# A planned encoder layer: one gate moved between two mixers, two heads kept on chip, and the last product's order changed

## The chip, the cores and the metric

The kernel runs on one core of a Trainium2 chip. Five engines work side by side, each through its own list of instructions in order: TensorE (PE, with its weight loads PEld), VectorE (DVE), ScalarE (ACT), GpSimd (POOL) and SyncE (SP), which here issues nearly all DMAs. The metric is the device time of one execution in microseconds (us), the median of several runs; lower is better.

## The reference

One layer is computed for 1024 prompt rows and 32 sample rows (T = 1056 columns in all), with 1024 channels, 8 heads of 64 in each of two mixers, and a feed-forward width of 4096:

```
z = rmsnorm(x) @ w_in                    # q, k, v of both mixers, indexer, two gates
o_a = softmax attention over the 256 best keys per row (mixer A)
o_b = stick-breaking attention (mixer B)
m = sigmoid(gate_a) * (o_a @ w_branch_a) + sigmoid(gate_b) * (o_b @ w_branch_b)
h = x + m @ w_out
y = h + square(relu(rmsnorm(h) @ w_up)) @ w_down
```

The outputs are y for both groups and the new keys and values.

## The kernel before

All matrix products are made to near full precision with three passes: a value is split into a high part and a low rest (on ACT a cast to the high part, on POOL or DVE a subtraction for the rest), and `three` (line 514) multiplies high by high, high by low and low by high. One 128 by 512 slab of weights is a unit: a DMA into `wst`, the cast to `wh`, the subtraction to `wl`.

**What sets the order.** The program is not written in the order in which it runs. Every call is recorded as a node; a planner (`Plan`) gives each node an estimated cost and issues on each engine, among the nodes that are ready by its reckoning, the one of the lowest rank: FAST, PREP, MAIN, FILL, SLOW. Matmuls of products are FILL, so that PE takes them only where the matmuls of attention aren't ready. What comes out is one fixed list for each engine; on the chip each list runs in order.

**The attention stage.** Mixer B's 8 heads come first, then mixer A's twice over: pass 0 for the first 512 rows, pass 1 for the other 512. For a 128-row tile PE multiplies q by k (bank `s`, three of them); mixer A then takes on DVE the masked maximum (which empties the bank), on ACT the exponential, on DVE the reciprocal of its sum, on POOL the scaling of `p`; PE transposes `p` (bank `t`), ACT and DVE split the transposed tile (`tt`), PE multiplies by v (bank `o`), and `halves` adds the two halves of the result into a tile `o`, which goes by DMA to `do` in DRAM. Mixer B uses sigmoids in place of the exponential.

**What fills PE there.** The 16 gates (8 for each mixer) are products of 72 matmuls each: 24 of 512 columns and 48 of 272 (`gate`). Four run before the stage, four at its start, and `GATES_BESIDE` says how many are recorded after each of mixer B's heads: six. The last two are in `self.raw`: they are recorded among mixer A's heads and stored without their sigmoid, which is taken later, where the gate is loaded again (`gated` and `merge`); so ACT needs no sigmoid between the exponentials of mixer A. Beside mixer A's heads stand 26 pieces of filling: the two raw gates and 24 branch products (`branch_b0`, `branch_b1`, `branch_a0`, 8 each), dealt out by `FILL_AHEAD` and `FILL_BESIDE`.

**The merge.** `load_o` brings the heads' results back from `do` in pairs of heads, splits them (cast on ACT, subtraction on POOL), and the branch products of the second half (`w_ba` by `xl`) follow, then `w_out`, then the feed-forward part.

**Down.** The last product takes seven forms of the hidden layer (B11, T1 to T4, B21, B22: a scheme of seven block products in place of eight), read back from `du` in DRAM. Its phases before are: B11 over all 16 blocks p; (T2, T3, B22) over blocks 0 to 7, then over 8 to 15, called here three-0 and three-1; B21 over all 16; (T1, T4) over 0 to 7 and over 8 to 15, called two-0 and two-1. In each phase q runs over 4 pairs of output rows. At q = 0 the phase loads its u (one DMA, cast and subtraction for each form and block), and keeps them until q = 3; there are 24 places for them (`slots`), taken in turn over the tiles ml, oa, xl and mh. B11 and B21 need 16, a three 24, a two 16. For each q and four blocks a three also makes three sets of weights from four loads (`us<-w_down`) by four additions and subtractions on DVE, while B11 and B21 just load a unit. `finish` multiplies a finished part of y by the norm and adds h, loaded into one of `self.hs` (4 places).

Of the kernel before, what the change touches and what calls it, by code (L numbers as in the profile page):

```python
# [28 lines left out]
H = 8  # L29
# [15 lines left out]
MIDS = 1  # L45
FILL_AHEAD = 1
GATES_BEFORE, GATES_FIRST = 4, 4
GATES_BESIDE = (1,1,1,1,1,1,0,0)
FILL_BESIDE = (0,1,1,1,2,2,2,2,2,2,2,2,2,2,2,1)
FWORDS = 2500  # L50
PA_BANKS = ('s', 'pj', 's', 's', 'pj')
TOPK = (("a", [2, 3, 4, 7], (7,), 0), ("b", [5, 6, 8], (5, 6), 16))
# [55 lines left out]
class Plan:  # L108
# [3 lines left out]
    def __init__(self, nc, tc):  # L112
        self.nc, self.tc = nc, tc
        self.tensor, self.vector = Issuer(self, PE, nc.tensor), Issuer(self, DVE, nc.vector)
        self.scalar, self.gpsimd = Issuer(self, ACT, nc.scalar), Issuer(self, POOL, nc.gpsimd)
        self.sync = Issuer(self, SP, nc.sync)
        self.either = Issuer(self, EITHER, nc)
        self.nodes, self.mem, self.rings = [], {}, {}
        self.members, self.banks, self.onchip = {}, set(), set()
        self.floors = {"left": 0.0, "right": 0.0, None: 0.0}  # L120
        self.free = [0.0] * 5
        self.now = [[] for _ in range(5)]
        self.later = [[] for _ in range(5)]
        self.pipe = 0.0
        self.port = {DVE: (0.0, 0.0), POOL: (0.0, 0.0)}
        self.table = None
        self.level = [2]
        self.hold = None
# [22 lines left out]
    def open(self, name, side="left", space=None):  # L151
        st = ExitStack()
        kw = {"space": space} if space is not None else {"side": side}
        if space is not DRAM:
            kw["reuse_waits"] = "tile"
        pool = st.enter_context(self.tc.tile_pool(name=name, bufs=1, **kw))
        p = (pool, st, side if space is None else None, name)
        self.members[name] = []
        return p

    def close(self, *pools):
# [7 lines left out]
    def tile(self, pool, shape, dtype, name, tag=None, bufs=1, fine=False):  # L169
        tag = tag or name  # L170
        kw = {} if pool[2] is None and pool[3].startswith("d") else {"tag": tag, "bufs": bufs}
        t = pool[0].tile(shape, dtype, name=name, **kw)
        words = 1
        for s in shape[1:]:
            words *= s
        if dtype in SMALL:
            words = -(-words * SMALL[dtype] // 4)
        if kw:
            ring = self.rings.setdefault((pool[3], tag), [])
            old = ring[-bufs].touched if len(ring) >= bufs else ()  # L180
            psum = pool[3].startswith("ps") and not fine
            m = Mem(1 if psum else 4, 1 if psum else words, old, self.floors[pool[2]])
            ring.append(m)
        else:
            m = Mem(1, words * shape[0])
        self.mem[t.tensor.name] = m
        if pool[3].startswith("ps"):
            self.banks.add(t.tensor.name)
        if kw:
            self.onchip.add(t.tensor.name)  # L190
        self.members[pool[3]].append(m)
        return t
# [267 lines left out]
class Layer:  # L460
# [732 lines left out]
        nc.vector.tensor_sub(tt[:m, 1, :n], pt[:m, :n], tt.bitcast(F32)[:m, 0, :n])  # L1193
        return tt

    def halves(self, po, o):

        nc = self.nc
        nc.scalar.copy(o, po[64:128])
        nc.vector.tensor_add(o, po[0:64], o)  # L1200

    def rooms(self, is_a):

# [3 lines left out]
    def attend(self, h, is_a, passes=(0, 1)):  # L1207

        nc, at = self.nc, self.att
        g = h if is_a else H + h  # L1210
        kk = nc.tile(at, [128, SEQ], F32R, "k", bufs=3)
        v = nc.tile(at, [128, 8, 128], F32R, "v", bufs=3)
        dk = self.dk[g].rearrange("s e t -> (s e) t")
# [25 lines left out]
        for i in passes:  # L1239
            o = nc.tile(at, [64, 512], F32, "o", bufs=2)  # L1240
            for t0 in (4 * i + 2, 4 * i):
# [8 lines left out]
                for j0 in range(0, t0 + 2, 2):  # L1250
# [6 lines left out]
                    for j in (j0, j0 + 1):  # L1257
                        lo = 128 if j > t0 else 0
                        s0 = 256 * (j - j0)
                        for z in range(2):  # L1260
                            nc.tensor.matmul(
                                po[:, lo:256], v[:, j], parts[:, z, s0:s0 + 256 - lo],
                                start=j + z == 0, stop=j + z == t0 + 2)
                self.halves(po, o[:, c:c + 256])
            with nc.rank(FAST):
                nc.sync.dma_start(self.do[g, :, 512 * i:512 * i + 512], o)
            self.mid = self.mid[1:] + [len(nc.nodes) - 1]

    def attend_new(self, u, is_a):
# [79 lines left out]
    def load_o(self, o, g, groups):  # L1349

        nc = self.nc
        for e in range(4):
            for i in groups:
                lo, hi = ((0, W1), (W1, T))[i]
                h, l = o[i][:, e], o[i][:, 4 + e]
                with nc.rank(PREP):
                    nc.sync.dma_start(
                        l.bitcast(F32), self.do[2 * g + 2 * e:2 * g + 2 * e + 2, :, lo:hi].rearrange("g e t -> (g e) t"))
                    nc.scalar.copy(h, l.bitcast(F32))
                    nc.gpsimd.tensor_sub(l, l.bitcast(F32), h.bitcast(F32))  # L1360

    def branch(self, name, e, o, done, parts):

# [272 lines left out]
    def down(self, late, form):  # L1636
# [4 lines left out]
        slots = self.ring([  # L1641
            v for z in homes for v in self.temps(flat(z), z.shape[1] * z.shape[2] // T, 0, T)])
        raws = self.ring(self.temps(late[0], 4, 0, 512) + self.temps(late[1], 4, 0, 512))
        self.hs = self.ring(self.temps(self.ft, 4, 0, 512))
        half = T // 2

        def raw(q, p, r, c):
# [55 lines left out]
                for r, c in ((1, 1), (0, 1), (1, 0)):  # L1703
                    d(r, c, True)

        for fs, weights, blocks, after in (
                ((B11,), one(0, 0), (range(16),), after1),
                ((T2, T3, B22), weights6, (range(8), range(8, 16)), after6),
                ((B21,), one(0, 1), (range(16),), after2),
                ((T1, T4), weights5, (range(8), range(8, 16)), after5)):  # L1710
            for b, block in enumerate(blocks):
                u = {}
                for q in range(4):
                    tags = [next(self.turn) for _ in fs]
                    ps = [[self.bank(t)[:, :n] for n, _ in QUADS] for t in tags]
                    for p0, ws in [(p0, weights(q, p0 // 4)) for p0 in range(block[0], block[-1], 4)]:
                        for f, w, bank in zip(fs, ws, ps):
                            wh, wl = w()
                            if q == 0:
                                u.update({(f, p): load(f, p) for p in range(p0, p0 + 4)})  # L1720
                            for i, (n, lo) in enumerate(QUADS):
                                cs = slice(i * 256, i * 256 + n)
                                with nc.rank(FILL):
                                    for s in range(4):
                                        ks = slice(s * 128, s * 128 + 128)
                                        uh, ul = (z[:, cs] for z in u[f, p0 + s])
                                        self.three(bank[i], wh[:, ks], wl[:, ks], uh, ul,
                                                   p0 + s == block[0], p0 + s == block[-1])
                    for i, (n, lo) in enumerate(QUADS):

                        def d(r, c, done=False, q=q, n=n, lo=lo):
                            cs = slice(lo + c * n, lo + c * n + n)
                            if done:
                                return self.finish(2 * q + r, cs)
                            return self.pick(self.yy, 2 * q + r, cs)

                        with nc.rank(FAST):
                            after(b, d, *(z[i] for z in ps))

    def finish(self, e, cs):  # L1740

# [93 lines left out]
```

## Time and profile before

| | |
|---|---|
| median of 3 runs | 1705.32 us (1704.97 to 1709.24) |
| the profiled execution's own time | 1703.88 us |
| its span, first to last instruction | 1702.1 us |
| PE busy | 1671.8 us (98%) |
| DVE, ACT, POOL busy | 1349.7, 942.4, 847.7 us |

In the rows further on, busy time of PE is modelled: a matmul's record lasts until its result is out, while the next one already runs, so a full PE still may not be at its fastest. The issue interval, from the start of one matmul to the start of the next, tells more. Every record names line 440, where the planner calls the operation, so the tiles tell the place: `s`, `t`, `o` are attention, `pj` with `xh` and `xl` a gate or a branch, `pj` with `og` a branch of the first half; `a`, `b`, `c` and `pj` are the four banks of the later stages.

### The profile page before, as it was taken

How to read it: one execution, taken by the hardware profiler on the slowest of the kernel's cores; microseconds unless marked ns; L12 is line 12 of the kernel's file. 1: busy time of each engine (PE TensorE's matmuls, PEld its weight loads, DVE VectorE, ACT ScalarE, POOL GpSimd, SP SyncE). 2: the span in 40 equal slices, each digit the busy share in tenths (PEclk: the TensorE clock that was granted, in tenths of full speed). 3: DMA queues.
4: the chain of work that ended last, by engine and by line, in shares of the span. 5: the costliest groups of instructions: out<-in, count | busy, mean ns of one | idle time of the engine just before them, and what ended most of it. 6: DMA issues, size and time to landing. Idle time of an engine off the chain costs nothing.

```text
span 1702.1 us, 34820 instructions
## 1 busy us (share of the span) xinstructions
PE 1671.8 (98%) x12242; PEld 1591.3 (93%) x12242; DVE 1349.7 (79%) x2846; ACT 942.4 (55%) x2019; POOL 847.7 (50%) x699
## 2 busy tenths in 40 slices
PE   8999999999999999899999999999999999999998
PEld 7998999999999998798999999999999999989998
DVE  8777899987477888876666549999988879888756
ACT  7556888764376776877754555333333544425431
POOL 5432332343386676456668648433333556656420
PEclk9999999999999999999999999999999999999999
DMA  7234453355573636778855644444443687756744
GB/s 257 83 104 125 140 154 121 103 157 149 156 213 94 188 97 166 197 237 241 241 178 160 182 122 134 156 140 140 140 150 130 225 274 237 271 161 235 252 131 149
DMA packets 182575, 289.00 MB, mean 170 GB/s; under 512 B 30976, under 2 KB 62176, under 8 KB 182400
## 3 DMA queue, kind: packets, MB, share of 16 engines
q1 hardware_dynamic: 182112, 286.43, 54.4%
q8 instruction: 97, 1.59, 0.4%
q14 instruction: 78, 0.64, 0.1%
q10 hardware_dynamic: 288, 0.34, 0.1%
HBM read 193.52 MB, written 93.07 MB: 168 GB/s over the span
## 4 chain that ended last, share of the span: by engine, by line
PE 85%; DVE 8%; issue 2%; DMA 2%; ACT 1%; POOL 1%; SPq 0%; DVEq 0%; ACTq 0%; POOLq 0%
PE pj L440 35%; PE c L440 11%; PE b L440 10%; PE a L440 10%; PE s L440 10%; PE o L440 5%; PE t L440 5%; DVE junk L440 2%; DVE y L440 1%; DVE mh L440 1%; DVE us L440 1%; POOL wl L440 0%; SPq L440 0%; DVE wl L440 0%; DVE small L440 0%
## 5 line engine op out<-in xcount | busy, mean ns | idle before, releaser
L440 PE MATMUL pj<-xl,wh 128*128 128x272 f32 (+2 forms) x1200 | 335.5, 312 | 0.0
L440 POOL TENSOR_TENSOR wl<-wst,wh 128x512 fp32r<-128x512 f32 x160 | 231.5, 1455 | 200.8 <-ACT wh L440 195.1
L440 PE MATMUL pj<-xh,wh 128*128 128x272 f32 (+1 forms) x768 | 251.6, 328 | 0.0
L440 PE MATMUL pj<-xh,wl 128*128 128x272 f32 (+1 forms) x768 | 250.8, 327 | 0.2 <-POOL wl L440 0.2
L440 PEld LDWEIGHTS pj<-xl,wh 128*128 128x128 f32 x1200 | 212.9, 188 | 10.5
L440 ACT CAST wh<-wst 128x512 fp32r<-128x512 f32 x213 | 130.4, 620 | 132.0 <-PE a L440 21.9
L440 PEld LDWEIGHTS pj<-xh,wl 128*128 128x128 f32 x768 | 144.5, 188 | 11.1 <-POOL wl L440 0.5
L440 PEld LDWEIGHTS pj<-xh,wh 128*128 128x128 f32 x768 | 144.6, 188 | 10.2 <-DVE gz L440 0.3
L440 POOL TENSOR_TENSOR p<-p,rem 128x383 f32<-128x383 f32 (+8 forms) x66 | 101.8, 1562 | 45.3 <-DVE rem L440 34.3
L440 DVE TENSOR_TENSOR tt<-t,tt 128x512 fp32r<-128x512 f32 (+2 forms) x168 | 101.4, 621 | 26.4 <-ACT tt L440 25.5
L440 POOL TENSOR_TENSOR wl<-y,wh 128x512 fp32r<-128x512 f32 x49 | 73.2, 1496 | 95.9 <-ACT wh L440 92.8
L440 DVE TENSOR_TENSOR_SCAN rem<-rem,first 128x384 f32<-128x384 f32 (+8 forms) x66 | 113.9, 1748 | 7.5 <-ACT rem L440 6.3
L440 ACT CAST tt<-t 128x512 fp32r<-128x512 f32 (+2 forms) x168 | 86.9, 539 | 42.0 <-PE t L440 34.6
L440 ACT CAST wh<-y 128x512 fp32r<-128x512 f32 x79 | 49.1, 622 | 105.9 <-issue 23.0
L440 ACT ACTIVATE junk<-score,cand 128x1024 bf16<-128x1024 f32 (+2 forms) x93 | 97.0, 1043 | 12.3 <-DVE cand L440 10.7
L440 PE MATMUL s<-k,q 128*128 128x512 f32 (+4 forms) x384 | 97.9, 353 | 5.6 <-DVE nb L440 3.0
L440 ACT CAST wh<-us 128x512 fp32r<-128x512 f32 x64 | 39.6, 622 | 114.1 <-PE pj L440 27.6
L440 PE MATMUL o<-tt,v 128*128 128x256 f32 (+1 forms) x640 | 98.4, 279 | 0.8 <-DVE o L440 0.4
L440 PEld LDWEIGHTS o<-tt,v 128*128 128x128 f32 x640 | 89.9, 189 | 6.3 <-DVE o L440 0.7
L440 DVE TENSOR_SCALAR_CACHE_REDUCE junk<-score,cand 128x384 bf16<-128x384 f32 (+1 forms) x124 | 92.9, 749 | 3.1
L440 PE MATMUL t<-ident,p 128*128 128x128 f32 (+1 forms) x596 | 90.9, 275 | 0.2 <-DVE tt L440 0.2
L440 POOL TENSOR_TENSOR wl<-us,wh 128x512 fp32r<-128x512 f32 x33 | 49.7, 1515 | 72.6 <-ACT wh L440 72.6
(359 smaller groups left out, 5610.3 us busy)
## 6 DMA issues: line engine op xcount, KB each, us to landing
us<-w_down SPq DMA_DIRECT2D x80, 256.0 KB, 3.0
q<-dq SPq DMA_DIRECT2D x64, 256.0 KB, 4.5
du<-y SPq DMA_DIRECT2D x56, 264.0 KB, 2.5
du<-us SPq DMA_DIRECT2D x56, 264.0 KB, 2.5
y<-w_up SPq DMA_DIRECT2D x44, 256.0 KB, 2.7
k<-dk SPq DMA_DIRECT2D x40, 256.0 KB, 5.0
v<-dv SPq DMA_DIRECT2D x40, 256.0 KB, 4.3
xl<-du SPq DMA_DIRECT2D x35, 264.0 KB, 5.2
```

Of the source, the lines that this page charges most:

```text
L440: fn(*args, **kw)
```

## The change

Four things, and what follows from them in the planner's lists:

1. `GATES_BESIDE` records a seventh gate beside mixer B's seventh head. It isn't raw any more, so its three sigmoids run where it is made. `FILL_BESIDE` deals out the 25 pieces that are left.
2. In pass 1 the last two heads of mixer A write their result with `halves` straight into an on-chip tile `last` (one of the three places of `v`), and `load_o` splits it from there; a DMA brings only its 32 sample columns. Two stores to `do` and one load of 544 columns go.
3. The planner reckons a PSUM tile's earliest time from when its pool was opened, no longer from when any other PSUM pool was closed.
4. In `down` the order is B11, three-0, B21, three-1, two-0, two-1, and h has nine places of 272 columns.

The matmuls are the same in number before and after, 12,240.

```diff
-GATES_BESIDE = (1,1,1,1,1,1,0,0)
-FILL_BESIDE = (0,1,1,1,2,2,2,2,2,2,2,2,2,2,2,1)
+GATES_BESIDE = (1,1,1,1,1,1,1,0)
+FILL_BESIDE = (1,1,1,1,1,2,2,2,2,2,2,2,1,2,2,1)
...
+        self.under[name] = self.floors[side if space is None else None]
...
-            m = Mem(1 if psum else 4, 1 if psum else words, old, self.floors[pool[2]])
+            m = Mem(1 if psum else 4, 1 if psum else words, old, self.under[pool[3]] if pool[3].startswith("ps") else self.floors[pool[2]])
...
-    def halves(self, po, o):
+    def halves(self, po, o, out=None):
...
-        nc.vector.tensor_add(o, po[0:64], o)
+        nc.vector.tensor_add(o if out is None else out, po[0:64], o)
...
+        direct = is_a and passes[0] == 1 and h >= H - 2
+        if direct and h == H - 2:
+            self.last = nc.tile(at, [128, SEQ], F32, "last", tag="v", bufs=3)
...
-                self.halves(po, o[:, c:c + 256])
-            with nc.rank(FAST):
-                nc.sync.dma_start(self.do[g, :, 512 * i:512 * i + 512], o)
+                self.halves(po, o[:, c:c + 256], self.last[h % 2 * HD:h % 2 * HD + HD, c:c + 256] if direct else None)
+            if not direct:
+                with nc.rank(FAST):
+                    nc.sync.dma_start(self.do[g, :, 512 * i:512 * i + 512], o)
...
+                x, old = l.bitcast(F32), 0
+                if g == 0 and i == 1 and e == 3:
+                    x, old = self.last[:, :T - W1], SEQ - W1
                 with nc.rank(PREP):
                     nc.sync.dma_start(
-                        l.bitcast(F32), self.do[2 * g + 2 * e:2 * g + 2 * e + 2, :, lo:hi].rearrange("g e t -> (g e) t"))
-                    nc.scalar.copy(h, l.bitcast(F32))
-                    nc.gpsimd.tensor_sub(l, l.bitcast(F32), h.bitcast(F32))
+                        x[:, old:], self.do[2 * g + 2 * e:2 * g + 2 * e + 2, :, lo + old:hi].rearrange("g e t -> (g e) t"))
+                    nc.scalar.copy(h, x)
+                    nc.gpsimd.tensor_sub(l, x, h.bitcast(F32))
...
-        self.hs = self.ring(self.temps(self.ft, 4, 0, 512))
+        self.hs = self.ring(self.temps(self.ft, 9, 0, 272))
...
-        for fs, weights, blocks, after in (
-                ((B11,), one(0, 0), (range(16),), after1),
-                ((T2, T3, B22), weights6, (range(8), range(8, 16)), after6),
-                ((B21,), one(0, 1), (range(16),), after2),
-                ((T1, T4), weights5, (range(8), range(8, 16)), after5)):
-            for b, block in enumerate(blocks):
+        three, two = ((T2, T3, B22), weights6, after6), ((T1, T4), weights5, after5)
+        for (fs, weights, after), b, block in (
+                (((B11,), one(0, 0), after1), 0, range(16)), (three, 0, range(8)),
+                (((B21,), one(0, 1), after2), 0, range(16)), (three, 1, range(8, 16)),
+                (two, 0, range(8)), (two, 1, range(8, 16))):
```

**Where the lists differ: ACT, where mixer A begins.** Before, one load of the exponential's table stands behind mixer B's last work, and then exponentials (`p,nb`), casts (`tt`) and copies (`o`) follow:

```order
L440 ACT_TABLE_LOAD
L440 ACTIVATE p,nb<-p,nb,fq 128x384
L440 COPY o<-o 64x256
L440 CAST tt<-t 128x512
L440 CAST tt<-t 128x384
L440 ACTIVATE p,nb<-p,nb,fq 128x512
L440 ACTIVATE p,nb<-p,nb,fq 128x128
L440 ACTIVATE p,nb<-p,nb,fq 128x256
```

In the changed list the moved gate's sigmoids (`gz`) come in between, behind the eighth exponential and twice more a little later:

```order
L441 ACTIVATE p,nb<-p,nb,fq 128x256
L441 ACT_TABLE_LOAD
L441 ACTIVATE gz<-gz 128x512
L441 CAST tt<-t 128x384
L441 CAST tt<-t 128x512
L441 ACT_TABLE_LOAD
L441 ACTIVATE p,nb<-p,nb,fq 128x384
L441 COPY o<-o 64x256
L441 CAST tt<-t 128x384 x2
L441 ACTIVATE p,nb<-p,nb,fq 128x512
```

Three sigmoids with a change of table before and after each: ACT's list has 12 table loads in place of 6, the six new ones all between mixer A's 8th and 15th exponential. The four casts of `og` for the first branch, which stood behind the 32nd exponential, stand between the 17th and the 18th.

**The same place on PE.** Before, attention alone up to the first raw gate:

```order
L440 MATMUL t<-ident,p 128x128 x8
L440 MATMUL s<-k,q 128x384 x2
L440 MATMUL s<-k,q 128x512 x2
L440 MATMUL s<-k,q 128x128 x2
L440 MATMUL o<-tt,v 128x256 x5
L440 MATMUL t<-ident,p 128x128 x2
L440 MATMUL o<-tt,v 128x256 x3
```

Now the moved gate's 72 matmuls lie among them, and the raw gate follows at once:

```order
L441 MATMUL t<-ident,p 128x128 x8
L441 MATMUL s<-k,q 128x512 x2
L441 MATMUL s<-k,q 128x128 x2
L441 MATMUL pj<-xh_103,wh_6914 128x512
L441 MATMUL pj<-xl_104,wh_6914 128x512
L441 MATMUL pj<-xh_103,wl_6915 128x512
L441 MATMUL pj<-xh_103,wh_6914 128x512
L441 MATMUL pj<-xl_104,wh_6914 128x512
L441 MATMUL pj<-xh_103,wl_6915 128x512
L441 MATMUL o<-tt,v 128x256
```

At the other end of mixer A, 47 matmuls of `branch_a0` stood behind the last matmul of attention; now 26 do, and 21 stand earlier, among the heads.

**SP, before three-1 in down.** Before, the 24 loads of u (`<-du`) for three-1 follow three-0's own weights (`us<-w_down`), since three-1 comes straight behind it:

```order
L440 DMA us_12756<-w_down 128x512
L440 DMA oa_12641<-du 128x528
L440 DMA us_12757<-w_down 128x512
L440 DMA oa_12641<-du 128x528 x3
L440 DMA xl_104<-du 128x528 x3
L440 DMA dw<-us_12757 128x512
L440 DMA xl_106<-du 128x528
L440 DMA us_12756<-w_down 128x512
L440 DMA xl_106<-du 128x528 x3
L440 DMA mh_12642<-du 128x528 x3
```

Now they lie within B21, the first eight of them in places that B21 doesn't use, between B21's stores of y and loads of h (`ft<-dh`):

```order
L441 DMA ml_12645<-du 128x528
L441 DMA oa_12641<-du 128x528
L441 DMA out_yT<-y_7215 128x272
L441 DMA oa_12641<-du 128x528 x2
L441 DMA us_12757<-w_down 128x512
L441 DMA ft<-dh 128x256
L441 DMA oa_12642<-du 128x528 x4
L441 DMA us_12757<-w_down 128x512
L441 DMA xl_104<-du 128x528 x3
```

## Rows read from the trace of the kernel before

**Rows 1.** The page's first part: busy time of PE, share of the span and count of instructions; PEld, DVE, ACT and POOL in the same line.

```profile
PE 1671.8 (98%) x12242; PEld 1591.3 (93%) x12242; DVE 1349.7 (79%) x2846; ACT 942.4 (55%) x2019; POOL 847.7 (50%) x699
```

**Rows 2.** Busy time by stretches of 50 us. The columns are the stretch, its length, then for PE, PEld, DVE, ACT and POOL the busy us and the count of instructions, the granted TensorE clock as a share, the busy share of the DMA engines, and GB/s. The stretches are the start of mixer A, its end and the merge, and three of down.

```profile
700.00:750.00 50.00, 46.15 (x312) 41.03 (x311) 40.62 (x165) 42.71 (x109) 29.81 (x40) 1.00 0.86 246
...
900.00:950.00 50.00, 50.00 (x324) 46.01 (x323) 34.72 (x46) 23.98 (x47) 44.32 (x38) 1.00 0.51 151
...
1450.00:1500.00 50.00, 47.76 (x386) 47.07 (x385) 43.06 (x52) 21.42 (x37) 33.31 (x20) 1.00 0.69 240
1500.00:1550.00 50.00, 48.00 (x379) 47.79 (x380) 36.14 (x50) 15.62 (x27) 20.47 (x14) 0.97 0.60 196
```

**Rows 3.** The same view for one stretch, the start of mixer A.

```profile
690.00:722.00 32.00, 27.73 (x187) 23.49 (x186) 28.38 (x122) 28.15 (x72) 13.58 (x24) 1.00 0.85 228
```

**Rows 4.** Groups of PE's instructions in that stretch, shapes apart: operands, shape and count | busy us, mean ns of one record | idle before and what ended it. Two matmuls of `pj` with 272 columns are left out.

```profile
L440 PE MATMUL t<-ident,p 128*128 128x128 f32 x63 | 9.1, 276 | 0.2 <-DVE tt L440 0.2
L440 PE MATMUL o<-tt,v 128*128 128x256 f32 x46 | 8.4, 300 | 0.4 <-DVE tt L440 0.3
L440 PE MATMUL s<-k,q 128*128 128x512 f32 x12 | 4.3, 423 | 0.0
L440 PE MATMUL s<-k,q 128*128 128x384 f32 x12 | 3.6, 384 | 3.3 <-DVE nb L440 3.0 <-DVE mx L440 0.2
L440 PE MATMUL s<-k,q 128*128 128x256 f32 x14 | 3.2, 313 | 0.3 <-DVE mx L440 0.3
L440 PE MATMUL o<-tt,v 128*128 128x128 f32 x16 | 2.7, 250 | 0.0
L440 PE MATMUL s<-k,q 128*128 128x128 f32 x12 | 2.2, 261 | 0.0
L440 PE MATMUL pj<-xh,wh 128*128 128x512 f32 x4 | 1.6, 409 | 0.0
L440 PE MATMUL pj<-xh,wl 128*128 128x512 f32 x3 | 1.2, 411 | 0.0
L440 PE MATMUL pj<-xl,wh 128*128 128x512 f32 x3 | 1.2, 395 | 0.0
```

**Rows 5.** PE's instructions in order of time, merged, in the same stretch: start, us, operands, shape, count. The starts of rows that follow each other give issue intervals.

```profile
694.89 2.10 PE L440 MATMUL o<-tt,v 128*128 128x256 f32 x16
696.83 1.06 PE L440 MATMUL t<-ident,p 128*128 128x128 f32 x8
697.64 1.22 PE L440 MATMUL s<-k,q 128*128 128x384 f32 x6
```

**Rows 6.** Pieces of the chain of waits in order of time (start, us, what): the branch matmuls of 512 columns behind the last head, and 24 matmuls of 272 columns in the next stage.

```profile
901.04 10.94 PE pj L440 x47
...
953.42 3.02 PE pj L440 x24
```

**Rows 7.** ACT's instructions in order of time around the start of mixer A: the last three sigmoids of a gate, then a cast, the load of the exponential's table and the first exponential.

```profile
677.55 0.62 ACT L440 ACTIVATE gz<-gz 128x512 f32<-128x512 f32 x1
...
682.93 0.43 ACT L440 ACTIVATE gz<-gz 128x272 f32<-128x272 f32 x1 [1.31 <-DVE gz L440]
...
690.75 1.07 ACT L440 CAST tt<-t 128x512 fp32r<-128x512 f32 x2
691.84 1.28 ACT L440 ACT_TABLE_LOAD   x1
693.14 0.71 ACT L440 ACTIVATE p<-p,nb,fq 128x384 f32<-128x384 f32 x1
```

**Rows 8.** The way of the last head's result in order of time: SP's store to `do`, ACT's cast and POOL's subtraction of what came back.

```profile
902.36 0.47 SPq L440 DMA_DIRECT2D do<-o  x1
...
908.04 0.63 ACT L440 CAST xl<-xl 128x544 fp32r<-128x544 f32 x1
...
908.75 1.37 POOL L440 TENSOR_TENSOR xl<-xl 128x544 fp32r<-128x544 f32 x1 [0.15 <-ACT xl L440]
```

**Rows 9.** SP in order of time: the four loads of `v` for mixer A's last two heads in pass 1, two for each head.

```profile
868.04 4.52 SPq L440 DMA_DIRECT2D v<-dv  x4
```

**Rows 10.** Busy time by stretches of 10 us in down, columns as in rows 2: behind the change from B11 to three-0, around the change from three-0 to three-1 (three rows), and behind the change from three-1 to B21.

```profile
1420.00:1430.00 10.00, 10.00 (x84) 10.00 (x83) 10.00 (x15) 2.72 (x5) 6.39 (x5) 1.00 0.40 113
...
1480.00:1490.00 10.00, 10.00 (x85) 10.00 (x84) 10.00 (x8) 7.51 (x14) 10.00 (x7) 1.00 0.87 330
1490.00:1500.00 10.00, 7.76 (x58) 7.07 (x56) 10.00 (x16) 0.48 (x1) 6.36 (x4) 1.00 0.33 101
1500.00:1510.00 10.00, 8.00 (x51) 7.79 (x52) 9.40 (x10) 2.60 (x5) 6.34 (x4) 0.83 0.59 184
...
1560.00:1570.00 10.00, 10.00 (x85) 10.00 (x84) 10.00 (x8) 6.25 (x11) 10.00 (x6) 1.00 0.49 176
```

**Rows 11.** Who waited for whom from 1484 to 1506 us (us in total, times, longest), around the same change.

```profile
ACT wh L440 <- DVE us L440: 13.2, 4, 9.8
...
PE c L440 <- ACT wh L440: 1.8, 1, 1.8
```

**Rows 12.** DVE and POOL in order of time there: the subtractions of loaded u, three on each engine; and an addition to y at the end of two-1.

```profile
1486.40 5.32 DVE L440 TENSOR_TENSOR mh<-mh 128x528 fp32r<-128x528 f32 x3
...
1489.36 5.27 POOL L440 TENSOR_TENSOR mh<-mh 128x528 fp32r<-128x528 f32 x3
...
1692.87 0.76 DVE L440 TENSOR_TENSOR y<-b,y 128x256 f32<-128x256 f32 x2 [4.90 <-PE b L440]
```

More of the change, by code (lines that the diff above doesn't have):

```diff
@@ L118, in __init__ @@
         self.nodes, self.mem, self.rings = [], {}, {}
-        self.members, self.banks, self.onchip = {}, set(), set()
+        self.members, self.banks, self.onchip, self.under = {}, set(), set(), {}
         self.floors = {"left": 0.0, "right": 0.0, None: 0.0}
@@ L1704, in after5 @@
                     d(r, c, True)
-        for fs, weights, blocks, after in (
-                ((B11,), one(0, 0), (range(16),), after1),
-                ((T2, T3, B22), weights6, (range(8), range(8, 16)), after6),
-                ((B21,), one(0, 1), (range(16),), after2),
-                ((T1, T4), weights5, (range(8), range(8, 16)), after5)):
-            for b, block in enumerate(blocks):
[L1712 to L1738, printed above, removed]
@@ new lines, in down, with d @@
+        three, two = ((T2, T3, B22), weights6, after6), ((T1, T4), weights5, after5)
[3 more added lines that the diff above has]
+                (two, 0, range(8)), (two, 1, range(8, 16))):
+            u = {}
+            for q in range(4):
+                tags = [next(self.turn) for _ in fs]
+                ps = [[self.bank(t)[:, :n] for n, _ in QUADS] for t in tags]
+                for p0, ws in [(p0, weights(q, p0 // 4)) for p0 in range(block[0], block[-1], 4)]:
+                    for f, w, bank in zip(fs, ws, ps):
+                        wh, wl = w()
+                        if q == 0:
+                            u.update({(f, p): load(f, p) for p in range(p0, p0 + 4)})
+                        for i, (n, lo) in enumerate(QUADS):
+                            cs = slice(i * 256, i * 256 + n)
+                            with nc.rank(FILL):
+                                for s in range(4):
+                                    ks = slice(s * 128, s * 128 + 128)
+                                    uh, ul = (z[:, cs] for z in u[f, p0 + s])
+                                    self.three(bank[i], wh[:, ks], wl[:, ks], uh, ul,
+                                               p0 + s == block[0], p0 + s == block[-1])
+                for i, (n, lo) in enumerate(QUADS):
+                    def d(r, c, done=False, q=q, n=n, lo=lo):
+                        cs = slice(lo + c * n, lo + c * n + n)
+                        if done:
+                            return self.finish(2 * q + r, cs)
+                        return self.pick(self.yy, 2 * q + r, cs)
+                    with nc.rank(FAST):
+                        after(b, d, *(z[i] for z in ps))
```

## The prediction

> **What bounds the kernel now.** First the page's busy shares: PE is busy for 98% of the span [rows 1], so nothing can come from the other engines but the time in which they keep PE waiting. The change neither adds nor removes a matmul, so its worth is the change in PE's lost time. Then the busy time by stretches of 50 us, to see where PE isn't full: the reader is to look for a PE below 50.00. Where the change works that is the start of mixer A (46.15) and the middle of down (47.76 and 48.00); at the end of mixer A and in the merge PE is full [rows 2]. These two places I looked at closely.
>
> At the **start of mixer A**, 690 to 722 us, ACT is busy for 28.15 and DVE for 28.38 of 32 us, PE for 27.73 [rows 3], and that flatters PE: the records overlap. I priced its matmuls by issue intervals. 16 of `o` take from 694.89 to 696.83, 0.121 us each; 8 transposes to 697.64, 0.101 each [rows 5]; 47 of 512 columns take 10.94, 0.233 each, and 24 of 272 take 3.02, 0.126 each [rows 6]. With the counts of rows 4: 63 transposes 6.4, 62 `o` 7.5, 50 `s` at the 512 column rate 7.2, ten `pj` and the two left out 2.6; 23.7 us of work in 32, so **8.3 us are lost**, 4.3 of them shown as idle. PE waits mostly at `s` for DVE's `nb` [rows 4]: a score bank comes free only behind DVE work that itself stands behind ACT's exponentials and casts. ACT and DVE set the pace there, since no filling is left.
>
> In **down**, a full PE issues 84 matmuls in 10 us. From 1490 to 1510 it issues 58 and 51 [rows 10]: 59 missing, 59 x 10/84 = **7.0 us**. In the second half the granted clock is 0.83 in the mean, so part ran at the lower level of 1.2 GHz after PE had waited; that is within the 7.0. Why: from 1480 DVE is full for 20 us, POOL for ten [rows 10], with the subtractions of the 24 loaded u of three-1, some 1.77 us each on either engine [rows 12]. DVE's work on the weights of three-1 stands behind them, ACT waits 13.2 us in total for it, and PE for ACT [rows 11].
>
> **The change, part by part. Down's order.** Two threes no longer follow each other. 24 subtractions at 1.77 us on two engines are 21 us of both. A place is freed only in q = 3 of the phase that used it, and the next phase wants it in its q = 0; q is 144 matmuls, 17 us, in a three, and 96, 11 us, in B21. Now three-0 is followed by B21, which needs 16 (14 us) and no reckoned weights; the same change, three-1 to B21, stands in the trace with both engines full and PE at 10.00 from 1560 to 1570 [rows 10]. Three-1 follows B21, with 8 of its 24 places free early; its likeness is B11 to three-0, PE 10.00 with 84 matmuls from 1420 to 1430, though DVE is full too [rows 10]. Three-1 to two-0 is 16 again, with half as much reckoning. So the 7.0 should go. What is late next: B11 hands its banks to ACT copies, B21 to DVE, an addition, a multiplication and an addition for each half, 6 x 0.38 = 2.3 us for each q [rows 12], in front of three-1's weights on a full DVE. Between 0 and 4.6 (two q's worth); the nearest row shows no loss, so I take 1.0. Down: **-6.0**. Nine places for h: at the end DVE waits for PE alone [rows 12], not for h, so 0; its loads move ahead on SP, among DMAs that nobody waits for there.
>
> **The moved gate.** 24 x 0.233 + 48 x 0.126 = 11.6 us of PE work come into the stretch that loses 8.3. But its sigmoids come with it. Before, the last cast ends at 691.82, the table load starts at 691.84 and the exponential at 693.14: 1.30 us for a change of table [rows 7]. Six new ones are 7.8, three sigmoids 0.62 + 2 x 0.43 = 1.5 [rows 7], together 9.3 us more on ACT, where everything queues: exponentials, the casts that PE's `o` needs, the copies that free bank `o`. The four `og` casts that moved up as well are only moved. If ACT sets the pace, the stretch grows by 9.3 and PE does 11.6 more in it: -2.3. If ACT's 3.85 us of idle [rows 3] take part of it in, up to -6.2, and -8.3 is all there is. Above, if the gate's matmuls don't lie where PE waits, +9.3. I take **-2.3**, the sum with ACT as the limit, since ACT and DVE are both near full in the row.
>
> On a change of table the Trainium skill speaks against this part: "ScalarE: Activation LUTs", section "What ACT_TABLE_LOAD costs", gives 1283 ns for the load and some 1380 ns to drain ACT before, 2.66 us in all. By it ACT would get 16.0 + 1.5 and this part would be +5.9. The trace has the first figure and not the second: 0.02 us lie between the cast and the load [rows 7].
>
> **The last two heads on chip.** Before, the last head's result is stored from 902.36, cast at 908.04 and subtracted until 910.12 [rows 8], some 9.1 us behind the last attention matmul at 901.04, under 10.9 us of branch matmuls [rows 6]; PE loses nothing [rows 2]. Now 26 matmuls are left, 26 x 0.233 = 6.1, and nine of the next product that don't need this result, 1.1: 7.2 us of cover. The way is 1.3 until the result is there (as before the store), a cast 0.63 and a subtraction 1.37, and at most one other operation ahead on each, 3.3 to 5.2 us. So 0; without that cover, as through DRAM, 9.1 - 7.2 = 1.9. The 21 matmuls, 4.9 us, go among the heads, in place of some of the gate's. `last` takes a place of `v`, so the last heads' loads start a place later: half of the 4.52 us that four take [rows 9], 0 to 2.3; 0, as those 4.9 us lie there. The planner's new reckoning of PSUM only picks another bank first in the merge, where PE is full: 0.
>
> **Sum**, against the profiled execution's own 1703.88: -6.0 - 2.3 = -8.3, so 1695.6. The median is 1.4 above that execution, so **1697.0** beside 1705.3.
>
> **The rivals.** *ACT eats the gate.* The six table loads fall in the loop in which PE waits for DVE and DVE for ACT, and the gate's matmuls stand a few rows too early or late in PE's fixed list to fill anything. Then the head loses 9.3 more: 1705.3 - 6.0 + 9.3 = 1708.6, slower. It decides once more than 6.0 us of the new ACT work shows on PE, that is from five table loads on. For it: ACT at 28.15 of 32. Against: a list with 11.6 us more in it leaves ACT more time for each exponential. Chance 0.12, 0.05 of it beyond 1710.4.
>
> *Down's wait only moves*, to the change from B21 to three-1, since DVE is full there already and gets 2.3 us for each q more. Then down gives nothing and the head 2.3: 1703.0. Against: B11 to three-0. Chance 0.14.
>
> *The head fills wholly*, as the planner laid it out: 1705.3 - 7.0 - 8.3 = 1690.0. Chance 0.12.
>
> *A change of table costs twice its row*, because ACT must run empty first, which the single load in the row may not show: 15.6 + 1.5 - 11.6 = +5.5, so 1704.8. Chance 0.04. It is the page's rule above, whose own figure would give 1705.2.
>
> **How the numbers follow.** The forecast with its neighbours, gains from 3 to 12 us, has 0.58. About 0.3%, 5.1 us, is what a measurement of this kernel can tell from no change. Faster by more: 0.53 of the forecast and 0.12, 0.65. Within: 0.05 of the forecast, 0.07 of ACT's case, 0.14, and most of the last rival, 0.27. Slower by more: 0.08. The range runs from the wholly filled head, 1690.0, to 1706.0, over down's rival and the double price, and leaves out the slower case and a little below.
>
> **What the profile after would show.** Down: no 10 us with fewer than 80 matmuls around either end of three-1, and a granted clock of 1.00 until the end. Start of mixer A: 12 table loads in ACT's list, each 1.28 us with 0.02 before it, and PE's lost time by the same reckoning 6 us, not 8.3; if it is 15 or more, ACT ate the gate. End of mixer A: 26 branch matmuls and no idle PE behind them, no store to `do` there. The prediction is wrong if PE waits elsewhere: for `v` in the last two heads, or among mixer A's later heads because the 11.6 us of filling are missed there.

## The result, and the profile after

| | before | after |
|---|---|---|
| median | 1705.19 us (5 runs, 1703.87 to 1709.24) | 1697.75 us (5 runs, 1695.57 to 1699.20) |
| profiled execution, its span | 1703.88, 1702.1 us | 1696.43, 1694.6 us |

The ratio of after to before is 0.9947, with a 95% interval of [0.9934, 0.9961]; a second measurement of the same kernel, told below, gave 0.9970 [0.9958, 0.9981]. By these two ratios the change is worth 5 to 9 us; 1697.0 us was forecast.

The page's first line, of after, answers to [rows 1]: the same number of matmuls (12242 in both traces, two more than the count given with the change), 5.6 us less busy time of PE, 6.6 us more of ACT.

```profile
PE 1666.2 (98%) x12242; PEld 1588.7 (94%) x12242; DVE 1350.5 (80%) x2847; ACT 949.0 (56%) x2025; POOL 848.9 (50%) x698
```

Busy time by stretches of after, columns as in [rows 2], in this order: the start of mixer A ([rows 3]), the four stretches of [rows 2], a longer stretch of mixer A's start, all of down, and three 10 us pieces of down (as [rows 10]): B11's start, B21's start and three-1's start.

```profile
690.00:722.00 32.00, 30.54 (x221) 28.17 (x219) 23.40 (x95) 28.89 (x60) 9.44 (x17) 1.00 0.71 200
700.00:750.00 50.00, 47.33 (x340) 43.69 (x338) 36.65 (x141) 45.21 (x102) 24.64 (x34) 1.00 0.83 236
900.00:950.00 50.00, 50.00 (x335) 46.55 (x334) 34.73 (x49) 24.22 (x50) 40.52 (x36) 1.00 0.50 152
1450.00:1500.00 50.00, 49.62 (x407) 49.41 (x406) 43.01 (x42) 23.72 (x39) 37.65 (x23) 1.00 0.71 244
1500.00:1550.00 50.00, 48.29 (x396) 48.08 (x396) 40.85 (x52) 20.50 (x34) 25.19 (x17) 1.00 0.69 232
...
692.00:732.00 40.00, 38.37 (x265) 34.88 (x264) 28.44 (x108) 37.93 (x79) 15.30 (x22) 1.00 0.76 220
...
1340.00:1690.00 350.00, 344.51 (x2812) 343.03 (x2811) 281.41 (x382) 139.14 (x241) 173.67 (x107) 1.00 0.67 225
...
1370.00:1380.00 10.00, 7.71 (x63) 7.49 (x62) 9.93 (x8) 2.19 (x4) 8.43 (x5) 1.00 0.80 270
...
1490.00:1500.00 10.00, 9.62 (x79) 9.41 (x78) 9.38 (x8) 1.24 (x2) 8.83 (x6) 1.00 0.44 137
...
1540.00:1550.00 10.00, 8.29 (x68) 8.08 (x67) 9.96 (x10) 3.49 (x6) 8.20 (x6) 1.00 0.55 183
```

At mixer A's start PE does 221 matmuls in 32 us, before 187; ACT is busy for 37.93 of 40 us there. In down the hole of 58 and 51 matmuls is gone, and the granted clock stays at 1.00 from 1340 to 1690. But 5 matmuls of 84 are missing where B21 begins, 16 (1.9 us) where three-1 begins, and B11's start has a larger hole than before. Who waits for whom (us in total, times, longest): PE at B11's start in before and in after (first two rows), then in after from 1538 to 1552 (two rows, as [rows 11]), and PE from 690 to 760.

```profile
PE a L440 <- DVE wl L440: 1.2, 1, 1.2
...
PE a L441 <- POOL wl L441: 2.3, 1, 2.3
...
ACT wh L441 <- DVE us L441: 14.1, 5, 8.6
...
PE c L441 <- ACT wh L441: 1.7, 1, 1.7
...
PE s L441 <- DMA q<-dq: 1.0, 1, 1.0
PE pj L441 <- ACT wh L441: 1.0, 1, 1.0
PE o L441 <- ACT tt L441: 0.5, 1, 0.5
```

The last three rows stand in the place of PE's waits for DVE's `nb` [rows 4]. The pair `ACT wh <- DVE us` is the one of [rows 11], now where B21 ends and three-1 begins.

The last head's subtraction on POOL, and PE's matmuls behind the 26th branch matmul, in order of time in after. The first matmuls of the next product, from 907.47, use other heads; the second matmul of the last row is the first one that waits for POOL's subtraction. The way through DRAM of [rows 8] took until 910.12.

```profile
905.41 1.38 POOL L441 TENSOR_TENSOR xl<-last,xl 128x544 fp32r<-128x544 f32 x1
...
907.47 0.41 PE L441 MATMUL pj<-xl,wh 128*128 128x272 f32 x2
...
908.60 0.42 PE L441 MATMUL pj<-xl,wh 128*128 128x272 f32 x2
```

**Lost time.** To compare kernels I took, from the one trace of each, every matmul's interval to the next one's start, less the median interval of the matmuls of its form, and added up the differences by stretch. What comes out holds both PE's waits and the matmuls that ran at a lower clock. Before loses 44.9 us in the whole program, after 37.0: 7.9 less, against 7.5 of span. "A starts" is 685 to 760 us, "merge" from the last matmul of attention to 1040, "B11 starts" 1340 to 1400, "inner" the changes of phase from 1470 to 1580; the times and ratios are those of the runs, each against the kernel before measured beside it.

| kernel | A starts | merge | B11 starts | inner | median us | ratio |
|---|---|---|---|---|---|---|
| before | 8.7 | 0.4 | 3.0 | 7.3 | 1705.2 | 1 |
| after | 3.9 | 1.5 | 4.1 | 2.9 | 1697.8 | 0.9947 |
| after, again | 5.3 | 0.9 | 5.6 | 2.9 | 1698.6 | 0.9970 |
| down's order only | 8.0 | 0.4 | 4.0 | 2.8 | 1704.0 | 0.9993 |
| all but down's order | 3.8 | 0.3 | 2.9 | 7.2 | 1701.4 | 0.9984 |
| gate only | 4.7 | 5.6 | 2.9 | 8.0 | 1706.9 | 1.0013 |
| gate and last heads | 6.3 | 0.9 | 3.0 | 7.8 | 1701.1 | 0.9975 |
| after, gate raw | 1.9 | 3.7 | 5.6 | 3.0 | 1696.5 | 0.9956 |
| after, table loads doubled | 7.9 | 0.3 | 4.1 | 2.8 | 1701.7 | 0.9976 |
| after, four places of h | 4.6 | 1.6 | 2.9 | 2.8 | 1694.7 | 0.9934 |
| after, u on DVE | 5.9 | 0.3 | 2.4 | 0.3 | 1694.3 | 0.9939 |
| after, all on DVE | 4.2 | 1.7 | 2.1 | 0.3 | 1691.4 | 0.9926 |
| before, all on DVE | 8.5 | 1.3 | 1.4 | 1.7 | 1697.0 | 0.9954 |
| after, raw and all on DVE | 1.7 | 3.9 | 2.0 | 0.3 | 1690.6 | 0.9915 |

Two executions of after differ by 1.4 at mixer A's start and 1.5 at B11's: smaller differences there say nothing. "Inner" repeats within 0.2 for the new order, within 0.8 for the old, as long as POOL has its share. Later heads of mixer A lose 2.2 to 4.9 in every kernel, with and without the gate.

The 1.5 at B11's start is the clock and not a wait. PE waits equally long for `wl` in both executions of after, 2.3 us; behind it the granted clock stays at 1.00 in the first and falls to 0.70 in the second, with 31 matmuls in 5 us in place of 43:

```profile
1380.00:1385.00 5.00, 5.00 (x43) 5.00 (x42) 4.20 (x6) 1.82 (x5) 1.59 (x1) 1.00 1.02 343
...
1380.00:1385.00 5.00, 5.00 (x31) 5.00 (x31) 2.70 (x4) 0.89 (x2) 0.07 (x1) 0.70 1.00 353
```

### The profile page after: what moved, and what is told of

The parts are those of the page before. It is cut to its first block, busy times and chain, and to the rows that moved or that the text cites. A ratio compares the mean times of both kernels' runs of the same rounds, so it can differ in the third digit from the quotient of the medians.

```text
span 1694.6 us, 34797 instructions
## 1 busy us (share of the span) xinstructions
PE 1666.2 (98%) x12242; PEld 1588.7 (94%) x12242; DVE 1350.5 (80%) x2847; ACT 949.0 (56%) x2025; POOL 848.9 (50%) x698
## 4 chain that ended last, share of the span: by engine, by line
PE 83%; DVE 7%; DMA 4%; issue 2%; POOL 2%; ACT 1%; SPq 0%; ACTq 0%; DVEq 0%; POOLq 0%
PE pj L441 34%; PE b L441 11%; PE c L441 10%; PE a L441 10%; PE s L441 10%; PE t L441 4%; PE o L441 4%; DVE junk L441 2%; DVE y L441 1%; POOL wl L441 1%; DMA oa<-du 1%; DVE xl L441 1%; DMA wst<-w_bb 0%; DMA xt<-x 0%; DVE small L441 0%
## 5 line engine op out<-in xcount | busy, mean ns | idle before, releaser
L441 POOL TENSOR_TENSOR wl<-wst,wh 128x512 fp32r<-128x512 f32 x163 | 238.1, 1467 | 201.2 <-ACT wh L441 192.1
```

Of the source, the lines that this page charges most:

```text
L441: fn(*args, **kw)
```

## Experiments: the parts of the change

**Down's order only.** The kernel before with parts of the last two hunks of the diff.

```diff
-        self.hs = self.ring(self.temps(self.ft, 4, 0, 512))
+        self.hs = self.ring(self.temps(self.ft, 9, 0, 272))
...
-        for fs, weights, blocks, after in (
+        three, two = ((T2, T3, B22), weights6, after6), ((T1, T4), weights5, after5)
+        for (fs, weights, after), b, block in (
...
```

> The kernel before with down's new order and the nine places of h alone. The forecast's term for down, -6.0, gives 1699.2 us. The trace of the changed kernel has less: there PE loses 4.2 us less than before around three-1's two ends (0.8 and 2.1 left of 7.1) and 1.1 more at the start of B11, so -3.1 to -4.2 and 1701.0 to 1702.1, if the 1.1 belongs to down's order or not. If the order gave the whole gain and the gate nothing, 1697.7. If down gave nothing (its wait only moves), 1705.2.

0.9993 [0.9981, 1.0005]: by time alone it can't be told from no change. Its lost time is that of after: inner 2.8, B11's start 4.0. So the trace gives 4.5 - 1.1 = 3.4 us, just outside the interval's 3.2. The times give 1.2. The traced execution was one of only two of the twelve at a granted clock of 1.000 (1699.29 and 1699.69 us); the other ten had 0.996 to 0.999 and took 1701.5 to 1707.8. So the 3.4 leans high: it counts this kernel without what it loses at a lower clock.

**All but down's order.** The changed kernel with down's old order and its four places of h.

```diff
-        self.hs = self.ring(self.temps(self.ft, 9, 0, 272))
+        self.hs = self.ring(self.temps(self.ft, 4, 0, 512))
...
-        three, two = ((T2, T3, B22), weights6, after6), ((T1, T4), weights5, after5)
-        for (fs, weights, after), b, block in (
...
+        for fs, weights, blocks, after in (
...
```

> The changed kernel with down's old order and its four places of h: gate, last heads and planner alone. The forecast's term for the head, -2.3, gives 1702.9. By the issue intervals of the changed kernel's trace the stretch from mixer B to mixer A's end lost 5.5 less than before, which gives 1699.7. If down gave the whole gain, 1705.2. The wait between three-0 and three-1 should stand in this profile as in that of before, some 7 us.

0.9984 [0.9975, 0.9992], 2.7 us, with down's old wait back at 7.2 and 5 us less lost at mixer A's start. Later heads of mixer A lost 4.9 in this trace and 2.5 in the one of before, so half of the 5 us doesn't show in the sum.

**The gate only**, and the gate with the last heads on chip (`halves` and `load_o` as in after, the planner as before). Of the gate only, the whole edit:

```diff
-GATES_BESIDE = (1,1,1,1,1,1,0,0)
-FILL_BESIDE = (0,1,1,1,2,2,2,2,2,2,2,2,2,2,2,1)
+GATES_BESIDE = (1,1,1,1,1,1,1,0)
+FILL_BESIDE = (1,1,1,1,1,2,2,2,2,2,2,2,1,2,2,1)
```

> The kernel before with the moved gate and its new dealing of the filling alone, the last heads through DRAM and the planner as before. If the gate is the whole of what the head gains, the same time as the kernel without down's order, between 1699.7 and 1702.9, and no idle PE where the last heads' results come back, since 26 matmuls still cover them. If the way through DRAM isn't covered by 26 branch matmuls, some 1.9 more than that kernel, with idle PE behind the last branch matmul of the first half.

> The kernel before with the gate's move and the last two heads on chip, without the planner's new reckoning of PSUM and without down's order. The gate alone gave 1.0013, and its profile has a wait of 3.83 us in the merge, for a POOL subtraction of weights queued behind four additions to ft. If the way of the last heads through DRAM made that wait, it is gone here and the ratio is that of all but down's order, 0.9984. If the planner's reckoning is what moved that subtraction, the wait stays and the ratio is 1.001.

1.0013 [1.0000, 1.0026] and 0.9975 [0.9963, 0.9987]: the gate alone gains nothing. PE's wait in the merge, in the gate-only kernel (905 to 930 us):

```profile
PE pj L440 <- POOL wl L440: 3.7, 1, 3.7
```

ACT, POOL and, last, PE's 5 us behind the wait (columns as in [rows 2]) there:

```profile
907.87 0.65 ACT L440 CAST xl<-xl 128x544 fp32r<-128x544 f32 x1 [2.37 <-DMA xl<-do]
908.42 4.28 ACT L440 CAST mh<-y 128x512 fp32r<-128x512 f32 x8
912.60 1.67 ACT L440 CAST wh<-wst 128x512 fp32r<-128x512 f32 x3
...
911.28 1.82 POOL L440 TENSOR_TENSOR xl<-xl 128x544 fp32r<-128x544 f32 x1
914.61 3.83 POOL L440 TENSOR_TENSOR ft<-ft,y 128x272 f32<-128x272 f32 x4 [1.51 <-DVE ft L440]
918.40 4.58 POOL L440 TENSOR_TENSOR wl<-wst,wh 128x512 fp32r<-128x512 f32 x3
...
920.00:925.00 5.00, 5.00 (x29) 5.00 (x30) 5.00 (x8) 0.62 (x1) 3.92 (x3) 0.70 0.63 188
```

The same casts and subtractions in the kernel with the last heads on chip:

```profile
906.94 1.12 ACT L440 CAST wh<-wst 128x512 fp32r<-128x512 f32 x2
907.97 4.27 ACT L440 CAST mh<-y 128x512 fp32r<-128x512 f32 x8
...
911.35 3.45 POOL L440 TENSOR_TENSOR wl<-wst,wh 128x512 fp32r<-128x512 f32 x2
914.76 4.07 POOL L440 TENSOR_TENSOR ft<-ft,y 128x272 f32<-128x272 f32 x4
```

The last head's subtraction comes 9.4 us behind the last matmul of attention (901.9), under 26 branch matmuls. POOL is busy until then and doesn't wait for it. What the way through DRAM changes is the lists: ACT waits 2.37 us for the load and casts the next `wh` behind eight casts to `mh`, and the `wl` that PE needs next stand on POOL behind four additions that wait 1.51 for DVE. In the kernel with the last heads on chip two `wh` stand ahead of the eight casts and two `wl` ahead of the four additions, PE waits for nothing from 905 to 930, and the two kernels are 6.5 us apart (0.0038 x 1705). Of the 5.6 that the gate-only kernel loses in the merge 3.7 are this wait, and most of the rest is the clock, 0.70 behind it. So the gate's filling, taken from the end of mixer A, gains only where the last heads stay on chip. The planner's reckoning of PSUM adds nothing that can be told: 0.9984 [0.9975, 0.9992] with it, 0.9975 [0.9963, 0.9987] without.

**The changed kernel again.**

> The changed kernel once more, beside the kernels of this call. The parts alone gave 0.9993 (down's order) and 0.9984 (all but down's order), which multiply to 0.9977, while the changed kernel gave 0.9947 with [0.9934, 0.9961]. If the parts add, it comes out near 0.9977 here and the first ratio was a lucky one; if they help one another (down's first waits depend on where the stages ahead of it end), near 0.9947 again.

0.9970, between the first measurement's 0.9947 and the parts' 0.9993 x 0.9984 = 0.9977. The parts' product lies within its interval; nothing asks for parts that help one another.

## Experiments: what the table loads cost

**The gate raw**, so that ACT has six table loads, not twelve.

```diff
+        late = []
...
-                    self.gate(next(gates), "gz", 3)
-        self.raw = list(gates)
-        fill = [(lambda e: self.gate(e, "gz", 3, True), e) for e in self.raw]
+                    e = next(gates)
+                    late += [e] * (h == 6)
+                    self.gate(e, "gz", 3, h == 6)
+        fill = list(gates)
+        self.raw = late + fill
+        fill = [(lambda e: self.gate(e, "gz", 3, True), e) for e in fill]
```

> The changed kernel with its moved gate stored without its sigmoids, which are taken later with those of the two gates treated so before: the same filling at mixer A's start, six table loads in place of twelve, 9.3 us less on ACT there. If ACT sets the pace there, most of the 3.9 us that PE still loses go: 1694 to 1695. If the filling covers ACT's extra work, the same time as the changed kernel, 1697.7, and the same lost time. If the later sigmoids cost more than the table loads, above 1699.

**Table loads doubled**: 18 of them in place of 12. `twice` is set for the moved gate, and `w` is one column that nobody reads.

```diff
...
+            if twice and n < 512:
+                for f in (AF.Exp, AF.Sigmoid) * 2:
+                    nc.scalar.activation(w, z[:, :1], f)
...
```

> The changed kernel with six more table loads at mixer A's start (18 in ACT's list in place of 12): behind two of the moved gate's sigmoids stand two exponentials and two sigmoids of one column each, written to a column that nobody reads. ACT gets 7.8 us for the loads and some 2 for the eight small operations. If ACT sets the pace at mixer A's start, most of it shows: PE loses 5 to 10 us more in that stretch and the time is 1704 to 1708. If the gate's filling covers it, the time is within 2 us of the changed kernel's.

Raw: 0.9956 [0.9943, 0.9968], no different from after; mixer A's start loses 1.9, but the merge 3.7 and B11's start 5.6, there with the clock at 0.75 behind the wait (1375 to 1380). Doubled: 0.9976 [0.9966, 0.9985]; mixer A's start loses 7.9. Over the eight kernels with the seventh gate and its sigmoids, that stretch loses 4.8 in the mean (3.8 to 6.3), and over the two raw ones 1.8. So 9.3 us off ACT give back 3.0, and some 9.4 more on it (6 x 1.30 + 8 x 0.20) cost 3.1: about a third, neither of the two ends. From 692 to 732, in the kernel with twice the loads, as the row of after above:

```profile
692.00:732.00 40.00, 34.65 (x228) 31.31 (x227) 23.30 (x88) 34.58 (x65) 10.35 (x15) 0.96 0.76 201
```

ACT is less busy there than in after, 34.58 to 37.93, and part of the loss is the clock, 0.96. The planner makes a new list for each of these kernels, so the third is what these lists show and not the price of ACT's time by itself. ACT in order of time in after, around the first two of the new loads:

```profile
702.31 0.20 ACT L441 ACTIVATION_READ_ACCUMULATOR p<-p,nb,fq 128x1 f32 x1
702.53 1.28 ACT L441 ACT_TABLE_LOAD   x1
703.82 0.63 ACT L441 ACTIVATE gz<-gz 128x512 f32<-128x512 f32 x1
704.58 1.02 ACT L441 CAST tt<-t 128x384 fp32r<-128x384 f32 x2
705.62 1.28 ACT L441 ACT_TABLE_LOAD   x1
706.91 0.71 ACT L441 ACTIVATE p<-p,nb,fq 128x384 f32<-128x384 f32 x1
```

There are 0.02 us before each load and 0.01 behind it, and so it is at all six new loads: the row's price holds for them. The Trainium skill ("ScalarE: Activation LUTs", section "What ACT_TABLE_LOAD costs") adds some 1380 ns of draining; no run here shows it.

## Experiments: what is left in down

DVE and POOL in order of time in after, ahead of three-1 (first DVE's rows, then POOL's):

```profile
1523.50 1.55 DVE L441 TENSOR_TENSOR y<-y,ft 128x256 f32<-128x256 f32 x1
1524.98 0.43 DVE L441 TENSOR_TENSOR y<-c,y 128x272 f32<-128x272 f32 x1
...
1531.44 1.82 DVE L441 TENSOR_TENSOR xl<-xl 128x528 fp32r<-128x528 f32 x1
...
1537.33 0.69 DVE L441 TENSOR_TENSOR mh<-mh 128x528 fp32r<-128x528 f32 x1
...
1523.18 4.81 POOL L441 TENSOR_TENSOR oa<-oa 128x528 fp32r<-128x528 f32 x3 [0.50 <-DMA oa<-du]
1527.94 8.23 POOL L441 TENSOR_TENSOR xl<-xl 128x528 fp32r<-128x528 f32 x5
```

The same DVE subtraction takes 1.82 us while POOL's five run (until 1536.17) and 0.69 after them. The addition to `y` from on-chip tiles takes 1.55 beside POOL, and 0.42 in the kernel whose down has no POOL (told next); the one that reads the bank `c` takes 0.43 beside POOL too. The Trainium skill, page "SBUF — State Buffer", section "Who interferes with whom", has this as a rule: a DVE instruction with two inputs in SBUF contends with a GpSimd one that reads SBUF, and the ports that they share are an exclusive lock. The trace agrees: the DVE subtraction from 1531.44 ends at 1533.26, 0.56 us behind the POOL one that ran beside it (until 1532.70), so most of its own 0.69 came only then.

**u on DVE** (first edit) and **all on DVE** (both).

```diff
-                nc.either.tensor_sub(l, l.bitcast(F32), h.bitcast(F32))
+                nc.vector.tensor_sub(l, l.bitcast(F32), h.bitcast(F32))
...
+        self.low = nc.vector
```

> The changed kernel with all subtractions of loaded u in down on DVE, none on POOL. In its trace a 128 by 528 subtraction takes DVE 0.69 us while POOL is idle and 1.8 while POOL subtracts beside it, and POOL 1.3 to 1.8: 24 of them are 21 us on both engines and 16.6 on DVE alone. If what is left of down's waits (2.46 us at the start of B11, 0.54 and 1.87 at the two ends of B21) comes from DVE and POOL slowing each other, these shrink and the time falls by 2 to 4 us, to 1694 to 1696. If it comes from how much DVE has to do, DVE now has more and they grow, 1698 to 1702.

> As the kernel with u on DVE, and the subtractions of down's weights on DVE as well, so that POOL does nothing in down. If the two engines slow each other, every subtraction of DVE takes 0.6 to 0.7 us here and down loses less than with u alone on DVE: 1693 to 1695. If DVE's own load decides, this is the slowest of the four, above 1700.

0.9939 [0.9925, 0.9953] and 0.9926 [0.9914, 0.9938]. Busy time with all on DVE, at both ends of B21 and in all of down:

```profile
1490.00:1500.00 10.00, 10.00 (x84) 10.00 (x83) 5.45 (x11) 2.48 (x4) 0.00 (x0) 1.00 0.72 205
1540.00:1550.00 10.00, 10.00 (x84) 10.00 (x83) 8.62 (x15) 2.08 (x4) 0.00 (x0) 1.00 0.74 245
...
1340.00:1690.00 350.00, 343.12 (x2810) 342.46 (x2808) 258.11 (x488) 139.86 (x241) 7.29 (x4) 1.00 0.67 226
```

DVE does 488 instructions in place of 382, nearly all of POOL's 107 among them, in 258 us in place of 281. PE has its 84 at both ends of B21, and what the inner changes lose falls from 2.9 to 0.3.

**Before, all on DVE**: the same two edits, with the old order.

> The kernel before, its old order of down kept, with all subtractions of down on DVE and none on POOL. If the wait between three-0 and three-1 was one of too much work next to itself, as the forecast argued (24 subtractions for one three), 24 x 0.69 us on DVE alone are 16.6 us against 17 us of PE for one q, and some of the 7 us stay, 3 or more: ratio 0.998. If what made it was DVE at 1.8 us a subtraction beside POOL, the 7 us go as they did by the new order, and the start of B11 gains 1 too: about 8 us less, ratio 0.995 to 0.996, without any reordering.

0.9954 [0.9941, 0.9966], as much as the whole change, with the phases in their old order. What is left where three-0 met three-1 ([rows 10], 58 and 51 matmuls):

```profile
1490.00:1500.00 10.00, 9.39 (x74) 8.95 (x74) 9.72 (x20) 2.62 (x5) 0.00 (x0) 1.00 0.33 109
1500.00:1510.00 10.00, 10.00 (x84) 9.94 (x83) 8.28 (x15) 2.60 (x5) 0.00 (x0) 1.00 0.68 212
```

That is 10 matmuls missing, 1.2 us of the 7.0.

**Four places of h**, where the changed kernel has nine.

```diff
-        self.hs = self.ring(self.temps(self.ft, 9, 0, 272))
+        self.hs = self.ring(self.temps(self.ft, 4, 0, 512))
```

> The changed kernel with h's four places of 512 columns as before. The nine places bring some loads of h forward on SP, and with them the planner gives the weights' subtraction for which PE waits 2.46 us at the start of B11 to POOL; with four places it stands on DVE, as in the kernel before, where that wait is 1.32. If the nine places are the cause of the 1.1 us that B11's start loses more, the wait is 1.3 here and the rest of down is unchanged: 1 us under the changed kernel, ratio 0.9965. If B11 loses it to something else, the wait stays at 2.4. If the nine places were needed, a wait for ft shows on DVE within B21 and the time is above the changed kernel's.

0.9934 [0.9921, 0.9947]. PE's wait at B11's start (1362 to 1382):

```profile
PE a L441 <- DVE wl L441: 1.1, 1, 1.1
```

The `wl` is DVE's again, the wait 1.1 and not 2.3, and DVE waits for no load of `ft`. With POOL's share in place, the five kernels with four places lose 2.9 to 3.0 at B11's start, the five with nine 4.0 to 5.6. So the nine places cost 1.1 us there, and more where the clock falls behind the longer wait. Its interval overlaps that of the first measurement of after and lies below that of the second.

**Raw and all on DVE**, the two edits together.

> The changed kernel with the moved gate stored without its sigmoid and with all of down's subtractions on DVE: the two edits that gained, together. With all on DVE the time was 1691.4 and down lost nothing at its inner changes; without the table loads mixer A's start lost 1.9 us in place of 3.9, but the merge and the start of B11 lost 3.7 more. If those losses are the price of the later sigmoids, 1691 to 1693; if the one at B11 came from POOL and DVE beside each other and goes, 1688 to 1690.

1690.63 us, 0.9915 [0.9902, 0.9929]: the best of all, 14 us under the kernel before, though by its interval not apart from all on DVE, and between the two forecasts. B11's start loses 2.0 in place of the raw kernel's 5.6; the merge's 3.9 stayed.

## Why the prediction was right

The places where PE's lost time goes were named rightly, and the total came out right by some luck: by the traces its two terms err in opposite ways.

- **Down, -6.0.** This term is the one that was mis-sized. The old wait went, as forecast: by the traces the 7.3 of the inner changes fell to 2.9. What is late next was taken at 1.0 and measured 2.9, inside its bounds of 0 to 4.6, so the rival in which the wait only moves holds for two fifths of it; and "nine places for h: 0" is wrong by 1.1. Together -3.3 to -3.4 by the traces, and by its own runs -1.2, at most -3.2. "No 10 us with fewer than 80 matmuls" failed, with 79 and 68; the clock of 1.00 until the end held in down in one execution of after, and not in the other (0.70). The step that was weaker than it looked is the choice of B11 to three-0 as the likeness for B21 to three-1.
- **Why down waited.** "24 subtractions at 1.77 us on two engines" took 1.77 as the price of a subtraction. It is the price beside the other engine; 24 on DVE alone take 24 x 0.70 = 17 us, less than the 21 of both. The rest of DVE's list there was slowed as well. With all on DVE and the old order 1.2 us of the 7.0 are left, so the order was one remedy, not the cause.
- **The head, -2.3.** By lost time mixer A's start goes from 8.4, the mean of three kernels without the gate (8.0 to 8.7), to 4.8, -3.6, inside the bounds (from 690 to 722, where the sign was 6, it loses 2.6 and 3.2 in the two executions of after, and 8.0 before); the runs with all but down's order gave -2.7, which can't be told from either. "ACT as the limit" is the step that failed in size: about a third of ACT's new work shows on PE, not all of it. The filling by itself is worth 6 to 7 us (raw), of which the sigmoids and their loads take 3 back; so even that didn't reach the 8.3 of the rival in which the head fills wholly. The rival in which ACT eats the gate, and the one with the double price, are out.
- **The last heads, 0.** Right: 26 branch matmuls, no idle PE behind them, `xl` ready at 906.79 and first needed at 908.7. The way took 5.4 us from the end of attention (901.37), just above the 3.3 to 5.2. The 1.9 for the way through DRAM was far too small: measured, 4.7 of lost time in the merge and 6.5 of time. The forecast priced the detour's own length, and not the weights that the planner's lists put behind it on ACT and POOL.
- **The planner's PSUM, 0, and the missed filling, 0.** Neither shows beyond the scatter; for the missed filling that scatter is 2.2 to 4.9, too wide to say more.
- **The chances.** The terms named for "within" come to 0.26 and most of 0.04, not 0.27, which leaves some 0.05 and not 0.08 for slower.

By lost time the parts come to -3.4 and -3.6, -7.0; the medians gave 7.4 and 6.0, and the parts' own runs 3.9. What stays open: why the merge loses 2 to 3 us more with a third raw gate. The raw kernel's trace shows where: from 905 to 935 PE waits 0.7 for ACT's `wh` and 1.1 for DVE's `ft`.

## What to carry to other kernels

Before two engines share a list of subtractions, compare one engine's duration alone with its duration beside the other: here two engines took longer than one, and moving the work to the engine that looked full made it emptier. Price a detour by what is queued behind it on each in-order engine, not by its own length. Where a total comes out right, test its terms: here taking POOL out of down, which was no part of the change, gained more on top of it than down's new order had, and the nine places, counted at nothing, cost 1.1.

## What the hardware showed that was not expected

DVE's subtraction of 128 by 528 from on-chip tiles took 0.70 us alone and 1.82 beside POOL, POOL's subtractions 1.3 to 1.8; DVE's additions that read one PSUM bank kept their 0.43. Handing DVE all of POOL's share of down cut DVE's busy time by 23 us of 281. Behind the same wait of PE of 2.3 us at B11's start the granted clock stayed at 1.00 in one execution of the changed kernel and fell to 0.70 over 5 us in another, which cost 1.5 us.
